# A decoder's expert layer: 96 gathered tokens on 128 partitions and 160 dense ones, in place of 128 and 128

## The chip, the cores and the metric

The kernel runs on one core of one Trainium2 chip. The metric is the device time of one launch in microseconds (us), the median of several runs. A profile of one execution shows the engines: TensorE (PE; its weight loads are PEld), VectorE (DVE), ScalarE (ACT), GpSimd (POOL) and SyncE (SP, which issues DMAs here). The 16 DMA engines serve two queues: SP's, with the weights, and GpSimd's, with the gathers.

## The reference, cut to what matters

Two decoder layers run over 256 tokens of width 1024. Each has four sequence mixers, a cross attention, and then the part that the change touches, product-key expert retrieval:

```python
def peer_ffn(h, w_q, sub_keys, expert_u, expert_v):   # on x = RMSNorm(h), 256 tokens
    q = (x @ w_q).reshape(t, 8, 2, 128)               # 8 heads, two half queries each
    s = einsum('thpd,hpkd->thpk', q, sub_keys)        # 16 lists of 128 scores per token
    s_top, i_top = top_k(s, 16)
    cand = s_top[:, :, 0, :, None] + s_top[:, :, 1, None, :]
    best_s, pos = top_k(cand, 16)                     # 16 of 16384 experts per head
    gate = softmax(best_s)
    act = gelu(x . expert_u[idx])                     # 128 rows of 4 KB per token
    return sum(act * gate * expert_v[idx])            # 128 more rows per token
```

A token so uses 128 of 16384 experts in each layer, a row of `expert_u` and a row of `expert_v` for each. Arithmetic is in float32.

## The kernel before, in words

Weights come through a `Stream`: units of 128 x 1024 floats (512 KB), loaded by SP into a ring of ten buffers. The first kind, the 154 units of projections per layer, is split into a rounded high part (ScalarE) and a low part (VectorE, the subtraction in `pump`), since each product is made of three rounded ones. The last 16 of them are the query projection of `peer`. The second kind, 128 units of `expert_u` and 128 of `expert_v` per layer, is used as it lands, in float32.

`peer(l)` treats the tokens in two ways. Tokens NG to 255 (NT of them) are dense: all 16384 experts are computed for them. `u_unit(j)` multiplies one up unit (stationary) with `xf` (moving, NT columns), `u_evac` puts the gelu into `Sx`, and `w_step` makes the weight of each expert for four tokens at a time, from two masks that a small matmul joins; `w_put` multiplies it into `Sx`. After 128 up units, `v_mm` runs 128 down units against `Sx`. The first NG tokens, one on each partition, are gathered: `issue()` has GpSimd fetch for each partition the row that `idx[:, n]` names, `g_step()` has VectorE multiply it with the token (`xg`) and sum, or, for rows of `expert_v`, scale and add it into `acc`. NS places take rows in turn, so a new gather waits for an old row to be used.

What is chosen comes from VectorE (`best`: two rounds of the eight largest of a list; `rects`: candidate sums; then masks that look up expert numbers). It is a generator, `retrieval()`. The program is written out in one order by a loop over 16 query units and 128 up units: after each unit a credit is added, and the generator is advanced until its `yield` values have used it up. So the yields set how far selection lies ahead of or behind the units in each engine's order, not when it runs: an engine runs its own list in order and waits for others through semaphores. From the first half's selection on, 0.85 `g_step`s are placed after each unit, and all others among the down units.

NG is 128 before: the first 128 tokens gathered, the last 128 dense. Lists of both halves are chosen first, 16 times two, then the candidates of the first half, then those of the second. When the last two units (HOLD) are done, `h` gets `acc` by one VectorE addition for the gathered tokens; the dense ones come back by transposes (`back_half`) and `resid`.

Of the kernel before, what the change touches and what calls it, by code (L numbers as in the profile page):

```python
# [46 lines left out]
NG = 128  # L47
NT = T - NG
NS = 12
# [12 lines left out]
class Stream:  # L62
# [3 lines left out]
    def __init__(self, nc, rawp, wp, lp, srcs):  # L66
        self.nc, self.srcs = nc, srcs
        self.pools = {"raw": (rawp, NRAW, F32), "whi": (wp, NHI, F32R), "wlo": (lp, NLO, F32R)}
        self.used = {"raw": [], "whi": [], "wlo": []}
        self.ring = ["raw"] * NRAW + ["wlo"] * NLO + ["whi"] * NHI  # L70
        self.more, self.turn = None, 0
        self.raw, self.hi, self.lo = {}, {}, {}
        self.a = self.b = self.c = self.i = self.done = 0
        self.start = {}
# [25 lines left out]
    def pump(self, hi, lo):  # L100
# [9 lines left out]
        while self.c < min(n, lo, self.b):  # L110
            if self.c not in self.start:
# [3 lines left out]
                self.nc.vector.tensor_tensor(t, self.raw.pop(self.c), self.hi[self.c].bitcast(F32), OP.subtract)  # L115
# [39 lines left out]
def decoder(ctx, tc, x, memt, wd, ut, pv, pu, fnb, prm, fing, skt, cst, idn, out, dbg=None, layers=L):  # L155
# [14 lines left out]
    S = Stream(nc, rawp, wp, wlp, units)  # L170

# [893 lines left out]
    def peer(l):  # L1065
# [17 lines left out]
        last, nsel = back, [0]  # L1083

        def own(n):
            if not nsel[0]:
                nsel.append(up.tile([128, 3664], F32, name="sel"))
            nsel[0] += n
            return nsel[1][:, nsel[0] - n:nsel[0]]
        sS = back(4096).rearrange("p (a b c) -> p a b c", a=2, b=16)  # L1090
        if NG == 128:
            back = own
# [12 lines left out]
        back = last  # L1105
# [8 lines left out]
        G.tensor_tensor(xf, xh.bitcast(F32)[:, :, NG:], xl.bitcast(F32)[:, :, NG:], OP.add)  # L1114
        xg = up.tile([128, D], F32, name="xg")
        acc = up.tile([128, D], F32, name="acc")
        G.dma_start(acc, fnb[l])
        defer(lambda: V.scalar_tensor_tensor(xg[:NG], h[:NG, 0], rs[:NG, 2:3], acc[:NG], op0=OP.mult, op1=OP.mult), 4)
# [5 lines left out]
        place = [rows[:NG, n] for n in range(NS - 4)]  # L1124

        def more_places():

            for n in ("xh", "xl"):
                t_ = xp.tile([128, 2, D], F32, name=n)
                place.extend(t_[:NG, i] for i in range(2))  # L1130
# [15 lines left out]
        def rects(lst, dst, p0, p1, o=0):  # L1146
            for a0, na, b0, nb in lst:
                ov = dst[:, :, o:o + na * nb]
                x0, x1 = p0[:, :, a0:a0 + na], p1[:, :, b0:b0 + nb]
                if na == 1:  # L1150
                    V.tensor_tensor(ov, x0.to_broadcast([128, 8, nb]), x1, OP.add)
                elif nb == 1:
                    V.tensor_tensor(ov, x0, x1.to_broadcast([128, 8, na]), OP.add)
                else:
                    V.tensor_tensor(ov.rearrange("p h (a b) -> p h a b", a=na),
                                    x0[:, :, :, None].to_broadcast([128, 8, na, nb]),
                                    x1[:, :, None, :].to_broadcast([128, 8, na, nb]), OP.add)
# [13 lines left out]

        def retrieval():


            for b in range(16):
                while scored["n"] <= b:
                    yield None
                best(*((sv[:, tt, b], su_[:, tt, b], sS[:, tt, b]) for tt in range(2)))
                yield 1.3
            for tt in range(2):  # L1180
                V.tensor_copy(si[:, tt], su_[:, tt])
                s4 = sv[:, tt].rearrange("p (h q) c -> p h q c", q=2)
                i4 = si[:, tt].rearrange("p (h q) c -> p h q c", q=2)
                V.tensor_scalar(i0s[:, tt], i4[:, :, 0], 128.0, None, op0=OP.mult)
                rects([(a, na, 0, nb) for a, na, nb, _ in CAND], cd, s4[:, :, 0], s4[:, :, 1])
                yield 1.2
                rects(PAYL, py, i0s[:, tt], i4[:, :, 1])
                yield 1.0
                for n in range(0, 8, 2):
                    best(*((bv[:, n + i], bp[:, n + i], cd[:, n + i]) for i in range(2)))  # L1190
                    V.tensor_copy(bf[:, n:n + 2], bp[:, n:n + 2])
                    yield 1.0

                    for h_ in (n, n + 1):
                        ms = []
                        for k0, nc_, m in ((0, NPAY, bm0), (8, NCAND, bm1)):
                            sh = [128, 8, nc_]
                            m = m.rearrange("p (k c) -> p k c", k=8)
                            ms.append((k0, nc_, m, sh))
                        for k0, nc_, m, sh in ms:  # L1200
                            V.tensor_tensor(m, pord[:, None, :nc_].to_broadcast(sh),  # L1201
                                            bf[:, h_, k0:k0 + 8, None].to_broadcast(sh), OP.is_equal)
                        for k0, nc_, m, sh in ms:
                            V.tensor_tensor(m, m, py[:, h_, None, :nc_].to_broadcast(sh), OP.mult)  # L1204
                        yield 1.5
                        for k0, nc_, m, sh in ms:
                            V.tensor_reduce(be[:, h_, k0:k0 + 8], m, AX.X, OP.add)  # L1207
                        yield 0.75
                V.tensor_scalar(bi, be, 1.0 / 128, -63.5 / 128, op0=OP.mult, op1=OP.add)
                V.tensor_scalar(bi, bi, 12582912.0, -12582912.0, op0=OP.add, op1=OP.add)  # L1210
                V.scalar_tensor_tensor(bf, bi, -128.0, be, op0=OP.mult, op1=OP.add)
                V.tensor_tensor(be, bv, bv[:, :, 0:1].to_broadcast([128, 8, 16]), OP.subtract)
                A.activation(be, be, AF.Exp)
                if not tt:
                    b2 = ga.rearrange("p (h c) -> p h c", h=8)
                    V.scalar_tensor_tensor(b2, bf, 128.0, bi, op0=OP.mult, op1=OP.add)
                    V.tensor_scalar(idx, ga, float(l * 16384), None, op0=OP.add)
                    more_places()
                    for _ in range(NS):
                        issue()  # L1220
                yield 0.9
                V.tensor_reduce(gs, be, AX.X, OP.add)  # L1222
                V.reciprocal(gs, gs)
                V.tensor_tensor(be, be, gs[:, :, None].to_broadcast([128, 8, 16]), OP.mult)
                yield 0.6
                if tt or NG < 128:
                    ps = four(wps())
                    for c, src in enumerate((bi, bf, be)):
                        PE.transpose(ps[:, c], src.rearrange("p h c -> p (h c)"), ident)
                if not tt:  # L1230
                    V.tensor_copy(gate, be.rearrange("p h c -> p (h c)"))
                if tt or NG < 128:
                    prog["wait"] = True
                    yield None
                    prog["wait"] = False
                if tt:
                    V.tensor_copy(slots[:, :, 128 - NG:], ps[:, :3])
# [356 lines left out]
```

## Time and profile before

| | us |
|---|---|
| median of 3 runs | 2436.06 |
| lowest, highest | 2434.64, 2437.12 |
| the profiled execution | 2435.94 |
| its span, first to last instruction | 2434.1 |
| TensorE (matmul) busy | 2123.2 |
| VectorE busy | 1680.4 |
| ScalarE busy | 846.8 |
| GpSimd busy | 705.5 |
| DMA moved | 711.29 MB |

Busy time of the whole span says little here, as the stages have different limits; the rows below go by stage. In them, a `f32` matmul of the program stands as two instructions, each with its weight load; one in rounded f32 as one. Names are the program's, with buffer numbers left out; one memory can carry several names (`whi`, `wlo` and `raw` are the ring's buffers, `xh` and `xl` also hold gathered rows).

### The profile page before, as it was taken

How to read it: one execution, taken by the hardware profiler on the slowest of the kernel's cores; microseconds unless marked ns; L12 is line 12 of the kernel's file. 1: busy time of each engine (PE TensorE's matmuls, PEld its weight loads, DVE VectorE, ACT ScalarE, POOL GpSimd, SP SyncE). 2: the span in 40 equal slices, each digit the busy share in tenths (PEclk: the TensorE clock that was granted, in tenths of full speed). 3: DMA queues.
4: the chain of work that ended last, by engine and by line, in shares of the span. 5: the costliest groups of instructions: out<-in, count | busy, mean ns of one | idle time of the engine just before them, and what ended most of it. 6: DMA issues, size and time to landing. Idle time of an engine off the chain costs nothing.

```text
span 2434.1 us, 41395 instructions
## 1 busy us (share of the span) xinstructions
PE 2123.2 (87%) x16010; PEld 1982.0 (81%) x16010; DVE 1680.4 (69%) x3591; ACT 846.8 (35%) x1729; POOL 705.5 (29%) x565
## 2 busy tenths in 40 slices
PE   8999999998888878778299999999989888887871
PEld 8898999898888877777299989998979888777771
DVE  7877776599766655455778777665997667454557
ACT  6756755531444200000067567554314442000000
POOL 1010000103443455555410100001045435555554
PEclk9999999999999999999699999999999999999996
DMA  6444455468999999999844544554689999999996
GB/s 209 151 156 156 156 176 179 143 221 332 409 409 409 408 409 409 409 409 409 319 165 158 159 147 160 174 182 149 241 334 408 408 408 408 409 409 409 409 409 265
DMA packets 195605, 711.29 MB, mean 292 GB/s; under 512 B 21712, under 2 KB 21968, under 8 KB 195152
## 3 DMA queue, kind: packets, MB, share of 16 engines
q1 hardware_dynamic: 120672, 434.47, 49.1%
q0 software_dynamic: 74736, 274.17, 28.5%
q8 instruction: 126, 2.06, 0.3%
q14 instruction: 71, 0.58, 0.1%
HBM read 707.51 MB, written 1.05 MB: 291 GB/s over the span
## 4 chain that ended last, share of the span: by engine, by line
PE 40%; DMA 39%; DVE 12%; issue 5%; POOL 2%; ACT 2%; DVEq 0%; POOLq 0%; SPq 0%; ACTq 0%
PE b L236 38%; DMA rows<-in_pv_dram,idx 14%; DMA wlo<-in_ut_dram 5%; DMA raw<-in_ut_dram 4%; DMA xh<-in_pv_dram,idx 4%; DMA whi<-in_ut_dram 3%; DMA xl<-in_pv_dram,idx 3%; DMA rows<-in_pu_dram,idx 3%; DVE acc L1270 3%; DVE sel L1170 1%; POOL rows L1251 1%; DVE sel L1201 1%; DVE sel L1204 1%; DVE rows L1261 1%; DVE sel L1207 1%
## 5 line engine op out<-in xcount | busy, mean ns | idle before, releaser
L107 ACT ACTIVATE whi<-raw 128x1024 fp32r<-128x1024 f32 x308 | 324.3, 1057 | 502.9 <-PE b L236 380.2
L115 DVE TENSOR_TENSOR wlo<-raw,whi 128x1024 fp32r<-128x1024 f32 x308 | 373.2, 1220 | 74.5 <-ACT whi L107 70.0
L1270 DVE SCALAR_TENSOR_TENSOR acc<-rows,aw,acc 128x1024 f32<-128x1024 f32 x168 | 215.8, 1285 | 174.1 <-DMA rows<-in_pv_dram,idx 172.9
L1251 POOL DMA_INDIRECT rows<-in_pu_dram,idx x176 | 213.3, 1212 | 396.7 <-DVE gs L1222 173.1
L236 PE MATMUL b<-xh,wlo 128*128 128x256 f32 x1120 | 317.4, 283 | 4.2 <-DVE wlo L115 4.0
L236 PE MATMUL b<-xh,whi 128*128 128x256 f32 x1120 | 321.0, 287 | 0.0
L236 PE MATMUL b<-xl,whi 128*128 128x256 f32 x1120 | 317.6, 284 | 1.0 <-DVE xl L313 0.9
L1251 POOL DMA_INDIRECT rows<-in_pv_dram,idx x168 | 226.0, 1345 | 178.7 <-DMA rows<-in_pv_dram,idx 75.2
L1261 DVE CUSTOM_DVE_ANT_0 rows<-rows,xg 128x1024 f32<-128x1024 f32 x176 | 213.3, 1221 | 60.9 <-DMA rows<-in_pu_dram,idx 60.9
L236 PE MATMUL b<-Sx,whi 128*128 128x128 f32 x1600 | 206.0, 282 | 52.4 <-DMA whi<-in_pv_dram 52.4
L236 PEld LDWEIGHTS b<-Sx,whi 128*128 128x128 f32 x1600 | 187.2, 192 | 71.0 <-DMA whi<-in_pv_dram 70.9
L236 PE MATMUL b<-xf,whi 128*128 128x128 f32 x1600 | 204.0, 286 | 43.7 <-ACT Sx L1336 27.2
L236 PEld LDWEIGHTS b<-xf,whi 128*128 128x128 f32 x1600 | 193.7, 200 | 51.6 <-ACT Sx L1336 28.0
L236 PEld LDWEIGHTS b<-xh,wlo 128*128 128x128 f32 x1120 | 214.5, 191 | 6.9 <-DVE wlo L115 6.9
L236 PEld LDWEIGHTS b<-xl,whi 128*128 128x128 f32 x1120 | 214.1, 191 | 1.9 <-DVE xl L313 1.7
L236 PEld LDWEIGHTS b<-xh,whi 128*128 128x128 f32 x1120 | 214.0, 191 | 0.5
L236 PE MATMUL b<-Sx,wlo 128*128 128x128 f32 x1248 | 162.0, 283 | 42.7 <-DMA wlo<-in_pv_dram 42.7
L285 POOL TENSOR_TENSOR rs<-rs,epsh 128x1 f32<-128x1 f32 x14 | 7.8, 555 | 658.8 <-DVE rs L283 658.8
L236 PEld LDWEIGHTS b<-Sx,wlo 128*128 128x128 f32 x1248 | 147.0, 193 | 57.5 <-DMA wlo<-in_pv_dram 56.0
L236 PE MATMUL b<-Sx,raw 128*128 128x128 f32 x1248 | 159.9, 282 | 38.6 <-DMA raw<-in_pv_dram 38.6
L236 PEld LDWEIGHTS b<-Sx,raw 128*128 128x128 f32 x1248 | 145.6, 192 | 52.8 <-DMA raw<-in_pv_dram 51.3
L257 ACT ACTIVATE Sx<-b 128x512 f32<-128x512 f32 (+17 forms) x100 | 40.1, 406 | 361.9 <-PE b L236 309.8
(316 smaller groups left out, 4354.8 us busy)
## 6 DMA issues: line engine op xcount, KB each, us to landing
raw<-in_wd_dram SPq DMA_DIRECT2D x308, 512.0 KB, 3.8
whi<-in_ut_dram SPq DMA_DIRECT2D x100, 512.0 KB, 20.4
whi<-in_pv_dram SPq DMA_DIRECT2D x100, 512.0 KB, 20.4
raw<-in_ut_dram SPq DMA_DIRECT2D x78, 512.0 KB, 19.9
wlo<-in_ut_dram SPq DMA_DIRECT2D x78, 512.0 KB, 20.4
raw<-in_pv_dram SPq DMA_DIRECT2D x78, 512.0 KB, 20.4
wlo<-in_pv_dram SPq DMA_DIRECT2D x78, 512.0 KB, 20.4
rows<-in_pu_dram,idx POOLq DMA_INDIRECT x176, 19.7
```

The lines of the kernel that those rows point to most:

```text
L107: self.nc.scalar.activation(t, self.raw[self.b], AF.Copy)
L115: self.nc.vector.tensor_tensor(t, self.raw.pop(self.c), self.hi[self.c].bitcast(F32), OP.subtract)
L236: PE.matmul(o, w, m, start=st, stop=sp)
L257: A.activation(o, i, AF.Copy)
L285: G.tensor_tensor(rs[:, 2 + tt:3 + tt], rs[:, tt:tt + 1], epsh[:, :1], OP.pow)
L1170: V.max_index(i[:, c], v[:, c], s)
L1201: V.tensor_tensor(m, pord[:, None, :nc_].to_broadcast(sh), bf[:, h_, k0:k0 + 8, None].to_broadcast(sh), OP.is_equal)
L1204: V.tensor_tensor(m, m, py[:, h_, None, :nc_].to_broadcast(sh), OP.mult)
L1207: V.tensor_reduce(be[:, h_, k0:k0 + 8], m, AX.X, OP.add)
L1251: G.indirect_dma_start(out=place[n % NS], out_offset=None, in_=src, in_offset=bass.IndirectOffsetOnAxis(ap=idx[:NG, n % 128:n % 128 + 1], ...
L1261: V.tensor_tensor_reduce(s, s, xg[:NG], 1.0, 0.0, OP.mult, OP.add, accum_out=act[:NG, k:k + 1])
L1270: V.scalar_tensor_tensor(acc[:NG], s, aw[:NG, k:k + 1], acc[:NG], op0=OP.mult, op1=OP.add)
```

## The change

NG becomes 96, so 96 tokens are gathered and 160 are dense. The gathered rows still come 128 at a time: partitions 96 to 127 take the last 32 of the 128 expert slots of tokens 0 to 95, in three groups of 32 tokens (`NX` = 3). So 96 gathers cover `expert_u` and 96 `expert_v`, in place of 128 and 128. `spread` copies the slots' numbers and gates over by small DMAs, `token_rows` copies the tokens, `acc` becomes three sums, and `add_sums` adds them to the right tokens by three matmuls with a constant (`join`) on top of the transposes. NS is 11. The selection tiles lie in the tail of `Sx`, no longer in a tile of their own, so that up units from the 53rd on need the selection done (`jsel`; it was 64).

The selection's order is new: lists of the first half, four heads at a time, each four followed by their candidates (`picks`); then the numbers of the first half, then lists and candidates of the second half. The yields have other values. In the query projection, the low parts of three units in four are made by GpSimd (`aside`), and `xf` is made by VectorE.

```diff
-NG = 128
+NG = 96
+NR = 128 - NG
+NX = NG // NR
 NT = T - NG
-NS = 12
+NS = 11
...
+                e = self.nc.gpsimd if self.c in self.aside else self.nc.vector
+                e.tensor_tensor(t, self.raw.pop(self.c), self.hi[self.c].bitcast(F32), OP.subtract)
...
+        q = l * (ND + 256) + ND - 16
+        S.aside.update(q + i for i in range(1, 16) if i % 4)
...
-        G.tensor_tensor(xf, xh.bitcast(F32)[:, :, NG:], xl.bitcast(F32)[:, :, NG:], OP.add)
+        V.tensor_tensor(xf, xh.bitcast(F32)[:, :, NG:], xl.bitcast(F32)[:, :, NG:], OP.add)
...
+        def token_rows():
+            V.scalar_tensor_tensor(xg[0][:NG], h[:NG, 0], rs[:NG, 2:3], xg[1][:NG], op0=OP.mult, op1=OP.mult)
+            for u in range(1, NX):
+                act_copy(xg[u][:NG], xg[0][:NG])
+            for u in range(NX):
+                G.dma_start(xg[u][NG:], xg[0][NR * u:NR * u + NR])
+        defer(token_rows, 4)
...
+        def spread(t_):
+            for u in range(NX):
+                G.dma_start(t_[NG:, NR * u:NR * u + NR], t_[NR * u:NR * u + NR, NG:])
...
+            for h0 in (0, 4):
+                for b in range(2 * h0, 2 * h0 + 8, 2):
+                    while scored["n"] <= b + 1:
+                        yield None
+                    lists(0, b)
+                    yield 3.4
+                yield from picks(0, h0, h0 + 4)
+            yield from numbers(0)
+            V.tensor_copy(h8(gate, 16)[:NG], be[:NG])
+            spread(gate)
+            prog["tt"] = 1
+            for b in range(0, 16, 2):
+                if b == 6:
+                    ps = turned(0)
+                if b == 10:
+                    V.tensor_copy(slots[:, :, :128 - NG], ps[:, :3, NG:])
+                lists(1, b)
+                yield 3.4
+            yield from picks(1, 0, 8)
+            yield from numbers(1)
+            yield 1.2
+            yield 1.2
+            yield 1.2
+            ps = turned(1)
+            yield 1.2
+            V.tensor_copy(slots[:, :, 128 - NG:], ps[:, :3])
+            prog["r"] = NT
+            prog["tt"] = 2
...
+            k = n % NG
+            G.indirect_dma_start(out=place[n % NS], out_offset=None, in_=pu if n < NG else pvr,
+                                 in_offset=bass.IndirectOffsetOnAxis(ap=idx[:, k:k + 1], axis=0))
...
+            u = k // NR
+            if n < NG:
+                V.tensor_tensor_reduce(s, s, xg[u], 1.0, 0.0, OP.mult, OP.add, accum_out=act[:, k:k + 1])
...
+                if k % NR == 0:
+                    V.tensor_scalar(acc[u], s, aw[:, k:k + 1], None, op0=OP.mult)
+                else:
+                    V.scalar_tensor_tensor(acc[u], s, aw[:, k:k + 1], acc[u], op0=OP.mult, op1=OP.add)
...
-            credit += 2.2 if not prog["tt"] else 1.1
+            credit += 2.2 if not prog["tt"] else 1.2
...
-        V.tensor_tensor(h[:NG, 0], h[:NG, 0], acc[:NG], OP.add)
...
+        def add_sums(b):
+            for u in range(NX):
+                mm(tb[b][0], join[:, u], acc[u][:, 512 * b:512 * b + 512], False, u == NX - 1)
```

On GpSimd, at the start of the first layer's `peer`, this stood before: the load of the sub keys, the making of `xf`, the load of the norm's gain, and then the gathers.

```order
L1109 DMA Sx<-in_skt_dram 128x2048
L1114 TENSOR_TENSOR xf<-xh,xl 128x1024
L1117 DMA acc<-in_fnb_dram 128x1024
L1251 DMA rows<-in_pu_dram,idx 128x1024 x8
L1251 DMA xh<-in_pu_dram,idx 128x1024 x2
```

Now there are the twelve low parts (`wlo`) and, among them, the copies of the tokens' rows; the copies of `idx` precede the first gather.

```order
L1106 DMA Sx<-in_skt_dram 128x2048
L1117 DMA xg_5318<-in_fnb_dram 128x1024
L1118 DMA join<-in_jn_dram 128x384
L118 TENSOR_TENSOR wlo<-raw,whi 128x1024 x3
L1125 DMA xg_5317<-xg_5317 32x1024
L1125 DMA xg_5318<-xg_5317 32x1024
L1125 DMA xg_5319<-xg_5317 32x1024
L118 TENSOR_TENSOR wlo<-raw,whi 128x1024 x9
L1142 DMA idx<-idx 32x32 x3
L1286 DMA rows<-in_pu_dram,idx 128x1024 x7
```

Twelve subtractions have come to this queue, ahead of every gather, and one addition has left it.

On VectorE, at the same place, the query units' low parts stood between the selection of lists before; `xl` is the last of the norm, and MAX, MAX_INDEX and MATCH_REPLACE belong to the lists.

```order
L313 SCALAR_TENSOR_TENSOR xl<-b_5268,pr,xh 128x256 x2
L115 TENSOR_TENSOR wlo<-raw,whi 128x1024 x4
L1118 SCALAR_TENSOR_TENSOR xg<-h,rs,acc 128x1024
L115 TENSOR_TENSOR wlo<-raw,whi 128x1024
L1168 MAX sel<-Sx 128x8 x2
L1170 MAX_INDEX sel<-sel,Sx 128x8 x2
L1166 MATCH_REPLACE Sx<-sel,Sx 128x128 x2
```

After the change the same place reads:

```order
L320 SCALAR_TENSOR_TENSOR xl<-b_5268,pr,xh 128x256 x2
L1111 TENSOR_TENSOR xf<-xh,xl 128x1280
L118 TENSOR_TENSOR wlo<-raw,whi 128x1024
L1121 SCALAR_TENSOR_TENSOR xg_5317<-h,rs,xg_5318 96x1024
L1181 MAX Sx<-Sx 128x8 x2
L1183 MAX_INDEX Sx<-Sx 128x8 x2
L1179 MATCH_REPLACE Sx<-Sx 128x128 x2
```

`xf` has come from GpSimd, and one low part in four is left.

On TensorE, at the end of the first layer, the last down units (`Sx,wlo`) were followed by transposes of the dense tokens (`idt,Sx`, line 1418) and the next layer's norm (line 304).

```order
L236 MATMUL b_8607<-Sx,wlo 128x128 x4
L1418 MATMUL b_10202<-idt,Sx 128x128 x4
L236 MATMUL b_8608<-Sx,wlo 128x128 x4
L1418 MATMUL b_10215<-idt,Sx 128x128 x4
L304 MATMUL b_10231<-idt,Sx 128x128 x2
```

Now the moving side of the units has 160 columns, the transposes are matmuls for both halves of the tokens, and the three sums are joined to them.

```order
L243 MATMUL b_8762<-Sx,wlo 128x160 x4
L243 MATMUL b_10233<-idt,Sx 128x128 x4
L243 MATMUL b_10238<-idt,Sx 128x128 x4
L243 MATMUL b_8763<-Sx,wlo 128x160 x4
L243 MATMUL b_10238<-xg_5317,join 128x512
L243 MATMUL b_10238<-xg_5318,join 128x512
L243 MATMUL b_10238<-xg_5319,join 128x512
L243 MATMUL b_10251<-idt,Sx 128x128 x4
L243 MATMUL b_10256<-idt,Sx 128x128 x4
L243 MATMUL b_10256<-xg_5317,join 128x512
L243 MATMUL b_10256<-xg_5318,join 128x512
L243 MATMUL b_10256<-xg_5319,join 128x512
```

Sixteen transposes' worth of matmuls and six joins stand where eight transposes stood.

## Rows read from the trace of the kernel before

**Rows 1.** Stages of layer 1: start:end us, width, busy us (count), clock, DMA, GB/s.

```profile
477.00:533.00 56.00, 54.20 (x441) 52.98 (x442) 49.45 (x216) 22.85 (x33) 6.65 (x3) 1.00 0.55 179
533.00:560.00 27.00, 27.00 (x245) 27.00 (x244) 26.08 (x160) 6.29 (x12) 0.00 (x0) 1.00 0.97 361
560.00:625.00 65.00, 51.02 (x404) 50.21 (x403) 63.87 (x234) 9.72 (x19) 29.31 (x27) 0.86 0.92 353
625.00:842.00 217.00, 197.63 (x1667) 190.06 (x1667) 147.10 (x359) 86.88 (x279) 91.82 (x79) 1.00 1.03 409
842.00:1170.00 328.00, 261.12 (x2045) 237.37 (x2044) 169.64 (x172) 1.03 (x4) 183.53 (x132) 1.00 1.03 409
1170.00:1208.00 38.00, 1.18 (x7) 0.59 (x5) 34.55 (x27) 2.66 (x4) 20.55 (x19) 0.54 0.89 349
1208.00:1221.00 13.00, 6.48 (x31) 5.87 (x31) 5.85 (x11) 4.63 (x13) 1.13 (x2) 0.64 0.12 41
```

**Rows 2.** Timeline of TensorE, first down units: start, length in us, what.

```profile
842.58 3.74 PE L236 MATMUL b<-Sx,whi 128*128 128x128 f32 x32
```

**Rows 3.** TensorE's groups by shape: stationary, moving, count, busy us, mean ns, idle.

```profile
L236 PE MATMUL b<-xh,wlo 128*128 128x256 f32 x1120 | 317.4, 283 | 4.2 <-DVE wlo L115 4.0
L236 PE MATMUL b<-wlo,xh 128*128 128x512 f32 x288 | 112.7, 391 | 0.0
L236 PE MATMUL b<-bb,aa 128*128 128x128 f32 x512 | 67.8, 275 | 0.5 <-ACT Sx L257 0.5
L236 PE MATMUL b<-cph,bch 128*128 128x128 f32 x4 | 0.9, 224 | 0.0
```

**Rows 4.** The page's costliest groups: the sums of gathered down rows on VectorE.

```profile
L1270 DVE SCALAR_TENSOR_TENSOR acc<-rows,aw,acc 128x1024 f32<-128x1024 f32 x168 | 215.8, 1285 | 174.1 <-DMA rows<-in_pv_dram,idx 172.9
```

**Rows 5.** Timeline of TensorE in the mixers: 256 columns, then 8 columns.

```profile
49.39 0.28 PE L236 MATMUL b<-xl,whi 128*128 128x256 f32 x1
49.51 0.28 PE L236 MATMUL b<-xh,wlo 128*128 128x256 f32 x1
49.63 0.51 PE L236 MATMUL b<-loga,ct 128*128 128x8 f32 x4
```

**Rows 6.** Waits in layer 1's expert part: total us, times, longest us.

```profile
PE b L236 <- ACT Sx L1336: 13.0, 2, 7.7
PE b L236 <- ACT gt L1339: 4.8, 8, 0.6
DVE Sx L1340 <- ACT gt L1339: 55.3, 34, 4.6
```

**Rows 7.** Timeline: picks of the first half begin, its indices, the first gather.

```profile
543.05 0.27 DVE L1181 CAST sel<-sel 128x256 f32<-128x256 uint32 x1
...
571.92 0.23 DVE L1217 TENSOR_SCALAR idx<-ga 128x128 uint32<-128x128 f32 x1
572.44 1.02 POOL L1251 DMA_INDIRECT rows<-in_pu_dram,idx  x1 [86.27 <-DVE gs L1222]
```

**Rows 8.** Timeline of layer 1's end: residual, next layer's first product.

```profile
1213.57 1.39 DVE L273 TENSOR_TENSOR h<-h,b 128x512 f32<-128x512 f32 x2
...
1220.95 0.36 PE L236 MATMUL b<-xh,whi 128*128 128x256 f32 x1
```

**Rows 9.** Timeline at the query's start: VectorE's subtractions beside GpSimd's addition.

```profile
479.90 3.48 DVE L115 TENSOR_TENSOR wlo<-raw,whi 128x1024 fp32r<-128x1024 f32 x3
...
480.14 5.51 POOL L1114 TENSOR_TENSOR xf<-xh,xl 128x1024 f32<-128x1024 f32 x1 [2.45 <-DVE xl L313]
```

**Rows 10.** VectorE's groups by shape, 625 to 842 us.

```profile
L1261 DVE CUSTOM_DVE_ANT_0 rows<-rows,xg 128x1024 f32<-128x1024 f32 x50 | 60.7, 1221 | 8.9 <-DMA rows<-in_pu_dram,idx 8.9
L1293 DVE TENSOR_SCALAR aa<-idt,slots 128x128 f32<-128x128 f32 x128 | 36.5, 359 | 0.0
...
L1261 DVE DVE_READ_ACCUMULATOR2_ANT act<- 128x1 f32 x77 | 6.4, 83 | 0.0
L1340 DVE TENSOR_TENSOR Sx<-Sx,gt 128x240 f32<-128x240 f32 x2 | 0.8, 409 | 3.3 <-ACT gt L1339 3.3
```

More of the change, by code (lines that the diff above doesn't have):

```diff
@@ L73, in __init__ @@
         self.a = self.b = self.c = self.i = self.done = 0
-        self.start = {}
+        self.start, self.aside = {}, set()
         for k, (_, whole) in enumerate(srcs):
@@ L170, in decoder @@
     S = Stream(nc, rawp, wp, wlp, units)
+    for l in range(layers):
+        q = l * (ND + 256) + ND - 16
+        S.aside.update(q + i for i in range(1, 16) if i % 4)
     h = base.tile([128, 2, D], F32, name="h")
@@ L1123, in peer @@
         rows = sp.tile([128, NS - 4, D], F32, name="rows")
-        place = [rows[:NG, n] for n in range(NS - 4)]
+        place = [rows[:, n] for n in range(NS - 4)]
         def more_places():
@@ L1129, in more_places @@
                 t_ = xp.tile([128, 2, D], F32, name=n)
-                place.extend(t_[:NG, i] for i in range(2))
+                place.extend(t_[:, i] for i in range(2))
+        def spread(t_):
+            for u in range(NX):
+                G.dma_start(t_[NG:, NR * u:NR * u + NR], t_[NR * u:NR * u + NR, NG:])
         scored = {"n": 0}
@@ L1146, in rects @@
         def rects(lst, dst, p0, p1, o=0):
+            n = dst.shape[1]
             for a0, na, b0, nb in lst:
@@ L1170, in best @@
                     V.max_index(i[:, c], v[:, c], s)
-        def retrieval():
[L1175 to L1237, printed above, removed]
-                    prog["r"] = NT
-                elif NG < 128:
-                    V.tensor_copy(slots[:, :, :128 - NG], ps[:, :3, NG:])
-                prog["tt"] = tt + 1
-                yield 0.5
@@ new lines, in numbers @@
+        def numbers(tt):
+            V.tensor_scalar(bi, be, 1.0 / 128, -63.5 / 128, op0=OP.mult, op1=OP.add)
+            V.tensor_scalar(bi, bi, 12582912.0, -12582912.0, op0=OP.add, op1=OP.add)
+            V.scalar_tensor_tensor(bf, bi, -128.0, be, op0=OP.mult, op1=OP.add)
+            if not tt:
+                V.scalar_tensor_tensor(h8(ga, 16)[:NG], bf[:NG], 128.0, bi[:NG], op0=OP.mult, op1=OP.add)
+                V.tensor_scalar(idx[:NG], ga[:NG], float(l * 16384), None, op0=OP.add)
+                spread(idx)
+                more_places()
+                for _ in range(NS):
+                    issue()
+            V.tensor_tensor(be, bv, bv[:, :, 0:1].to_broadcast([128, 8, 16]), OP.subtract)
+            A.activation(be, be, AF.Exp)
+            yield 1.2
+            V.tensor_reduce(gs, be, AX.X, OP.add)
+            V.reciprocal(gs, gs)
+            V.tensor_tensor(be, be, gs[:, :, None].to_broadcast([128, 8, 16]), OP.mult)
+            yield 0.6
@@ L1333, in u_evac @@
                 while prog["tt"] < 2:
-                    next(gen)
+                    next(gen, None)
             if tb < NT:
@@ L1428, in peer @@
                 back_half(0)
-        def whole(b, tt, over=None):
-            if tt or NG < 128:
-                resid(b, tt, tb[b][tt], scr, over)
-                return
-            square(junk[b], tt, b)
-            if b:
-                over(tt)
-        junk = [flat(ys[b])[:, :512] for b in range(2)]
+        add_sums(0)
+        back_half(1)
+        add_sums(1)
         for tt in (1, 0):
-            whole(0, tt)
-        back_half(1)
+            resid(0, tt, tb[0][tt], scr)
         def put(tt, r):
@@ L1497, in shape_constants, with joins @@
     return arr, np.ascontiguousarray(idn)
+def joins():
+    o = np.zeros((128, NX, 128), np.float32)
+    for u in range(NX):
+        for p in range(128):
+            o[p, u, p if p < NG else NR * u + p - NG] = 1.0
+    return o
 def lay_out(i):
```

110 lines of the change are left out of this document (66 added, 44 removed).

## The prediction

> **What bounds the kernel now.** I read the stages first [rows 1]: each layer's expert part has five. The query projection (477 to 533 us) keeps TensorE busy 54 of 56 us. Then come 128 up units and 128 down units of 512 KB, and beside them 256 gathers of 128 rows of 4 KB, again 512 KB each. From 625 to 1170 us the DMA engines are full, at 409 GB/s. The reader is to see that TensorE is not full there: in the down stretch (842 to 1170) it ran 2045 matmul instructions, 128 units of 16, so a unit took 328/128 = 2.56 us. That is 2 x 524,288 bytes at 409 GB/s: one unit and one gather, half the DMA each, although 2045 instructions need less. Next the timeline of that stretch [rows 2]: with its data there, TensorE does 32 instructions in 3.74 us; less the 0.275 us that the last one takes [rows 3], they start 3.465/31 = 112 ns apart, 1.79 us a unit. DMA therefore sets this stretch. Then 1170 to 1208: TensorE is at 1.2 of 38 us, VectorE at 34.6. About 27 gathered rows are left when the units end, and they are added up one at a time, 1.285 us each [rows 4]. 13 us later the next layer starts. The other layer repeats this within a few us.
>
> **The change, part by part.** Durations are from the profiled execution, 2435.9 us, 0.1 us below the median of 2436.06, so its sums are used as they stand.
>
> *Fewer gathers, wider matmuls.* 64 of 256 gathers go per layer: 64 x 1.28 = 82 us of DMA. The dense units now stream 160 columns, not 128. What an instruction of 160 columns costs is the largest term, and no row shows one. The 112 ns are not the columns': a matmul of 8 columns takes four instructions in 0.51 us, the last three also 112 ns apart [rows 5], so loading 128 x 128 weights sets it. So the cost could stay at 112. But an f32 instruction of 128 columns ends 275 ns after its start, like a rounded-f32 one of 256 columns (283), while a rounded one of 128 takes 224 [rows 3]. 256 columns more cost 391 - 283 = 108 ns. So f32 columns count double, and 128 of them need 108 ns, just under the weight load; 160 are 64 more column times, 27 ns, so 112 + 27 = 139 ns. From above: 256 single columns follow each other at 120 ns [rows 5], hence 120 + 27 = 147. I take 138.5, as 112 is already a ceiling for 128. A unit is then 16 x 138.5 = 2.216 us. (The Trainium skill, "FP8 and Floating Point Precision", TensorE Precision Notes, has true f32 in four passes through the array, two for each of the two instructions here. By that rule 139 holds and the time is the forecast; by the flat 112 it would be 2245. The lengths in rows 3 side with the rule, though none is of 160 columns.)
>
> *Up units.* 128 x 2.216 = 283.6 us. The dense tokens' weights come in groups of four: 40 groups for 160 tokens in place of 32, 8 instructions each, 40 x 8 x 0.112 = 35.8. TensorE's waits: today 13.0 us for ScalarE in two stalls, where an exponential stands in ScalarE's order before VectorE has its input, and 4.8 for evacuation [rows 6]. The new yields let the program run behind VectorE, so I take the 13 away. The 4.8 I raise to 7, since the groups are crowded into the last 73 units (now 88), and I put 3 on the second half's selection. Sum 329 us, against 842 - 533 = 309. DMA does not limit this stretch: 0.85 gathers and one unit are 2.37 us, TensorE needs 2.216 + 0.28.
>
> *When the selection must be done.* Its scratch lies in the last part of Sx, so all selection must be out before unit 53 is evacuated: TensorE gets there at 533 + 55 x 2.216 = 655. VectorE: candidate picks of one half take 572 - 543 = 29 us [rows 7]; for the first half, half of them now lie in the query stretch, so the gathers start about 533 + 14 + list work and index copies = 560, not 572. SP's unit loads share the DMA with them 12 us sooner, at 2.56 us a unit against TensorE's 2.216; the ring of 10 units carries that. In VectorE's order 28 gathered rows stand before the last 14 us of the second selection: 560 + 28 x 2.56 + 14 = 646. Nine us to spare, hence only 3 us of cost; from below 0, from above 20 if the gathers start late.
>
> *Down units.* The program consumes 0.85 rows a unit from the 37th of 144 units (query units counted) on: 91 by now. 11 are in flight, 90 are left. While they run, DMA splits as today: 90 x 2.56 = 230 us, in which 90 units land and up to 10 wait in the ring: 100, and TensorE would take 104. The other 28 go at 2.216: 62. Sum 292, I take 294 (ring empty 314, TensorE alone 284), against 328.
>
> *The end.* All gathers are in some 50 us before the last unit, so VectorE's chain goes and TensorE is late next. After its last unit come transposes as f32 matmuls, 16 instructions x 0.112 = 1.8, three joins of 512 f32 columns (1024 column times each instruction, 6 x 0.44 = 2.6), for both halves 8.8; then from the residual to the next layer 1220.95 - 1213.57 = 7.4 us as today [rows 8]. 16 us, against 1221 - 1170 = 51.
>
> *Low parts on GpSimd.* 12 of 16 query units per layer move. VectorE needs 1.16 us each, and it has 49 of 56 us to do there [rows 1, 9]. GpSimd's only op of this size took 5.51 us [rows 9]. At that, 12 are 66 us in a stretch of 56, and the query gets 15 us longer. But that op ran beside three VectorE subtractions that began before it and ended at 479.90 + 3.48 = 483.38; it ended at 485.65, 2.3 us later. I take 2.3: 27 us in 56, with a start 1.5 us later since the first is needed at once. Queued behind them on GpSimd are three row copies and the index copies, then every gather. (The Trainium skill, "SBUF — State Buffer", Who interferes with whom, says that a VectorE instruction with two SBUF inputs and a GpSimd one that reads SBUF fully block each other. By it the 5.51 is 3.2 of waiting and the time is the forecast, but VectorE's own picks will be held up by GpSimd too; with 5.5 as the op's own time it would be 2372.)
>
> *Sum per layer:* +1.5 +20 (329 - 309) -34 (294 - 328) -35 (16 - 51) = -47. Twice: 2436 - 94 = 2342 us. At 147 ns, 4096 instructions a layer add 33 us: -14, 2408. With the ring full and no waits, -67: 2302.
>
> **Rivals.** *VectorE becomes the bound after the selection.* All weight groups fall into the last 73 up units. VectorE has there 63 gathered rows x 1.30 = 82 us, 160 x 36.5/128 = 46 for the weights' masks, 76 products of half a us (0.41 in the row) = 38 [rows 10]: 166, and TensorE 198 + 7. Against: 40 us of room. For: VectorE waited 55.3 us for ScalarE's evacuation in 34 waits [rows 6]; if each of 36 pairs still costs 1.6 and gathers 14, VectorE takes 238, +33 a layer; with a selection 20 us late as well the layer is 6 us longer than before: 2448. It decides from 47 us a layer on.
>
> *Columns are free.* The instruction stays at 112 ns. Then DMA bounds: up units (128 + 102) x 1.28 = 295, down 230 + 28 x 1.79 = 280, end 16: 591 + 1.5 against 688, twice 95.5 less: 2245. Against it: 275 beside 224.
>
> *GpSimd needs 5.5 us.* +15 a layer: 2372. For it stands the row as printed; against it the 2.3 us.
>
> **How the numbers follow.** Forecast 0.68, own range 2302 to 2408, for the two prices of the instruction. VectorE bound 0.13, columns free 0.06, GpSimd slow 0.08 (inside the forecast's range), other 0.05. Range 2300 to 2420: it leaves out the free columns and most of the VectorE case. About 0.2% is what a measurement here can tell. Faster: 0.68 + 0.06 + 0.08 and a quarter of the rest, 0.86. Slower 0.12, same 0.02.
>
> **What would show it.** Dense instructions 139 ns apart: right; 112 or 147 and more: that term is wrong. GpSimd's subtractions near 2.3 us, the query under 60 us. No wait of TensorE at unit 53. TensorE busy nearly throughout up and down stretch, DMA under 409 GB/s in the last third of the down stretch, no VectorE chain at the end. Wrong would be: TensorE waiting for DMA through the down stretch, or for evacuation by more than 20 us in the up stretch.

## The result and the profile after

The changed kernel takes 2337.73 us, median of 4 runs (2336.17 to 2339.8), the kernel before 2435.84 in 4; the ratio is 0.9598, 95% interval 0.9581 to 0.9614. It is 98 us faster; forecast were 94 (2342 us, range 2300 to 2420). The total is right; the parts are less so:

| layer 1's expert part, us | before | forecast change | after | change |
|---|---|---|---|---|
| first up unit starts | 532.85 | +1.5 | 530.85 | -2.0 |
| up units | 309.9 | +20 | 323.3 | +13.4 |
| down units | 327.9 | -34 | 304.9 | -23.0 |
| end, to the next layer's first product | 50.5 | -35 | 11.1 | -39.4 |
| sum | | -47 | | -51 |

(In the kernel before, eight instructions of the last unit stand behind the chain of sums; they are counted with the end.) The other layer gained 46: up units 324.4, down units 305.6.

The stages of layer 1 after the change; the columns are those of [rows 1], with which they are to be compared.

```profile
476.50:531.00 54.50, 53.55 (x444) 52.93 (x443) 40.30 (x145) 24.82 (x36) 33.72 (x18) 1.00 0.60 205
531.00:566.00 35.00, 35.00 (x262) 35.00 (x261) 29.17 (x159) 6.03 (x11) 2.94 (x5) 1.00 0.87 287
566.00:660.00 94.00, 88.67 (x643) 87.98 (x642) 83.16 (x335) 15.81 (x32) 46.78 (x41) 0.97 1.02 404
660.00:854.00 194.00, 194.00 (x1483) 194.00 (x1482) 142.26 (x364) 101.35 (x309) 68.84 (x63) 1.00 0.99 377
854.00:1077.00 223.00, 215.29 (x1482) 202.38 (x1481) 117.91 (x100) 0.65 (x2) 126.23 (x91) 1.00 1.03 409
1077.00:1159.00 82.00, 81.16 (x587) 79.39 (x587) 12.06 (x11) 2.99 (x4) 0.00 (x0) 1.00 0.75 277
1159.00:1170.00 11.00, 8.67 (x44) 5.40 (x42) 4.38 (x9) 4.75 (x12) 1.30 (x2) 1.00 0.00 0
```

TensorE, the first busy column, is now busy nearly throughout, and its granted clock holds (0.86, 0.54 and 0.64 in the three stretches of [rows 1] in which TensorE stood idle, 0.97 at worst here). VectorE's chain at the end is gone: 4.38 us of work in the last 11, where it had 34.55 in 38. One stretch is still full of DMA with TensorE waiting in it: 854 to 1077, in which 215 of 223 busy us overstate TensorE: its 1482 instructions are worth 202 us at the 136 ns found below.

TensorE's timeline after the change: the stop at unit 53, then 64 dense instructions in one piece and the end of the layer.

```profile
656.06 0.80 PE L1244 MATMUL b<-idt,Sx 128*128 128x128 f32 x2 [4.26 <-DVE Sx L1224]
657.94 0.48 PE L1244 MATMUL b<-idt,Sx 128*128 128x128 f32 x1 [1.08 <-DVE Sx L1238]
...
1113.47 8.86 PE L243 MATMUL b<-Sx,whi 128*128 128x160 f32 x64
...
1155.86 1.95 PE L243 MATMUL b<-idt,Sx 128*128 128x128 f32 x16
1157.64 1.25 PE L243 MATMUL b<-Sx,wlo 128*128 128x160 f32 x8
1158.73 2.74 PE L243 MATMUL b<-xg,join 128*128 128x512 f32 x6
1161.30 1.95 PE L243 MATMUL b<-idt,Sx 128*128 128x128 f32 x16
1163.09 2.74 PE L243 MATMUL b<-xg,join 128*128 128x512 f32 x6
1168.16 1.94 PE L311 MATMUL b<-idt,Sx 128*128 128x128 f32 x16 [2.33 <-DVE Sx L301]
1170.00 0.38 PE L243 MATMUL b<-xh,whi 128*128 128x256 f32 x1
```

64 instructions of 160 columns in 8.86 us, less 0.30 for the last: 8.56/63 = 136 ns apart, forecast 138.5, where [rows 2] had 112 for 128 columns. The joins cost nearly what was forecast (six instructions of 512 columns in 2.74 us, forecast 2.6).

### The profile page after: what moved, and what is told of

The parts are those of the page before. It is cut to its first block, busy times and chain, and to the rows that moved or that the text cites. A ratio compares the mean times of both kernels' runs of the same rounds, so it can differ in the third digit from the quotient of the medians.

```text
span 2337.0 us, 41618 instructions
## 1 busy us (share of the span) xinstructions
PE 2280.6 (98%) x16216; PEld 2170.3 (93%) x16216; DVE 1545.3 (66%) x3483; ACT 890.7 (38%) x1813; POOL 591.5 (25%) x481
## 4 chain that ended last, share of the span: by engine, by line
PE 70%; DMA 21%; DVE 6%; ACT 1%; POOL 1%; issue 1%; SPq 0%; DVEq 0%; ACTq 0%; POOLq 0%
PE b L243 68%; DMA whi<-in_pv_dram 7%; DMA wlo<-in_pv_dram 5%; DMA raw<-in_pv_dram 3%; DMA xl<-in_pu_dram,idx 2%; DMA rows<-in_pu_dram,idx 2%; DMA xh<-in_pu_dram,idx 1%; DVE Sx L1212 1%; DVE Sx L1183 1%; DVE Sx L1215 1%; DVE Sx L1218 1%; PE b L509 0%; POOL rows L1286 0%; ACT whi L109 0%; DVE Sx L1181 0%
## 5 line engine op out<-in xcount | busy, mean ns | idle before, releaser
L1308 DVE SCALAR_TENSOR_TENSOR xg<-rows,aw,xg 128x1024 f32<-128x1024 f32 x120 | 154.2, 1285 | 140.7 <-DMA rows<-in_pv_dram,idx 140.2
L243 PE MATMUL b<-Sx,whi 128*128 128x160 f32 x1600 | 233.0, 302 | 5.8 <-DMA whi<-in_pv_dram 0.2
L243 PEld LDWEIGHTS b<-Sx,whi 128*128 128x128 f32 x1600 | 219.4, 190 | 18.0 <-DMA whi<-in_pv_dram 17.9
L243 PE MATMUL b<-xf,whi 128*128 128x160 f32 x1600 | 225.2, 299 | 0.0
L1286 POOL DMA_INDIRECT rows<-in_pv_dram,idx x122 | 166.7, 1366 | 142.4 <-DMA rows<-in_pv_dram,idx 60.8
L1286 POOL DMA_INDIRECT rows<-in_pu_dram,idx x126 | 140.5, 1115 | 220.3 <-DVE act L1297 137.7
L243 PE MATMUL b<-Sx,wlo 128*128 128x160 f32 x1248 | 181.8, 302 | 7.3 <-DMA wlo<-in_pv_dram 3.3
L264 ACT ACTIVATE Sx<-b 128x512 f32<-128x512 f32 (+21 forms) x116 | 43.2, 376 | 377.8 <-PE b L243 351.6
L243 PE MATMUL b<-Sx,raw 128*128 128x160 f32 x1248 | 181.4, 302 | 4.2
L243 PE MATMUL b<-xf,wlo 128*128 128x160 f32 x1248 | 180.5, 302 | 0.2 <-DMA wlo<-in_ut_dram 0.2
```

The costliest lines, as they stand in the source:

```text
L243: PE.matmul(o, w, m, start=st, stop=sp)
L264: A.activation(o, i, AF.Copy)
L1286: G.indirect_dma_start(out=place[n % NS], out_offset=None, in_=pu if n < NG else pvr, in_offset=bass.IndirectOffsetOnAxis(ap=idx[:, k:k + ...
L1308: V.scalar_tensor_tensor(acc[u], s, aw[:, k:k + 1], acc[u], op0=OP.mult, op1=OP.add)
```

## The experiments

All edits are to the changed kernel; its time is 2337.73, and "before" ran beside each at 2436 to 2438 us. The first four runs have one time each, the others five; a ratio is to "before", with its 95% interval. Only the first two leave something out, part of the output.

**What a column costs.** Two runs.

```
-                mm(ps[:, j % 2, :NT], unit[:, k], xf[:, k], k == 0, k == KC - 1)
+                w = 128 if k else NT
+                mm(ps[:, j % 2, :w], unit[:, k], xf[:, k, :w], k == 0, k == KC - 1)
...the down units in the same way; the other run with 144
```

128 columns: 

> The changed kernel, but of the 160 dense columns only 128 go through TensorE in the expert units (the first instruction pair of each accumulation excepted); the output of 32 tokens is left out. Gathers, selection and everything else stay. Columns theory (f32 columns count double, 112 ns of weight load is the floor): the instruction falls from 136 to 112 ns, TensorE is no longer the bound, DMA is: up stretch about 295 us (323 with 160 columns), down stretch 223 + 37 units x 1.79 = 290 (305), so 2337 - 2 x 43 = about 2250 us. Rival (the 136 ns come from something other than the number of columns, such as where the columns lie in Sx): instruction stays at 136, time stays at 2337.

144 columns: 

> The same with 144 columns (16 tokens left out). Columns theory, linear at 0.85 ns a column: instruction 122 to 124 ns; up stretch about 300 us, down stretch 297; about 2337 - 2 x 31 = 2275 us. Rival, a step rather than a slope: 136 ns as with 160 columns and 2337 us, or 112 ns as with 128 and the time of that run.

Measured: 2290.53 and 2295.54 us. TensorE's timeline in the down stretch, first with 128 columns:

```profile
1097.56 7.31 PE L243 MATMUL b<-Sx,whi 128*128 128x128 f32 x64
```

With 144:

```profile
1096.91 8.00 PE L243 MATMUL b<-Sx,whi 128*128 128x144 f32 x64
```

Less 0.28 for the last, over 63: 112 and 122.5 ns. With 136 for 160 columns that is a slope of 0.84 ns a column, and 112 at 128 where the slope alone would give 109: the columns theory, floor included. The times came out 40 and 20 us above the expectations, and the stages with 128 columns say why:

```profile
531.00:831.00 300.00, 284.00 (x2385) 277.28 (x2385) 254.29 (x859) 122.60 (x352) 121.67 (x108) 0.99 1.01 396
831.00:1053.00 222.00, 176.90 (x1377) 160.48 (x1377) 117.88 (x100) 0.22 (x1) 126.10 (x91) 1.00 1.03 409
1053.00:1135.00 82.00, 78.61 (x688) 77.28 (x689) 11.99 (x10) 2.88 (x4) 0.44 (x1) 1.00 0.85 312
```

The up stretch fell from 323 to 299 nearly as expected (295), but the down stretch stayed: 304.2 us against 304.9 (299.5 with 144 columns), although TensorE needs 24 ns less for each instruction. While gathers run, units land no faster than gathers do; a faster TensorE only waits longer (busy 177 of 222 us).

**How much room VectorE has.** Two runs.

```
+                    for _ in range(2):
                         V.tensor_scalar(aa[:, k], iota, slots[:, 0, t:t + 1], slots[:, 2, t:t + 1], ...)
...the other run with range(3)
```

Masks twice: 

> The changed kernel with every mask of the dense tokens' weights (128x128 on VectorE) made twice: 160 more instructions of 0.285 us, 46 us more of VectorE per layer, all after the selection. The prediction put the point from which VectorE decides at 47 us a layer; in the trace of the changed kernel VectorE is busy 142 of 194 us there, 52 us of room. Room theory: hardly longer, 0 to 10 us a layer from waits, 2337 to 2357 us. Rival (the order of VectorE's instructions, not the sum, decides: evacuations stand behind gathered rows): most of the 46 us show, 2337 + 2 x 35 = about 2405.

Masks three times: 

> The same with every mask made three times: 91 us more of VectorE per layer. Room theory: 91 - 52 = 39 us a layer and what the waits add, 2337 + 78 to 98 = 2415 to 2435 us. Rival with the order deciding: 2337 + 2 x 80 = about 2500.

Measured: 2368.07 and 2495.15 us. The stretch from the first weights to the last up unit, and TensorE's waits in it, masks twice:

```profile
660.00:868.00 208.00, 199.34 (x1492) 196.73 (x1492) 198.13 (x525) 99.04 (x316) 73.62 (x63) 0.99 0.95 350
```

```profile
PE b L243 <- ACT Sx L264: 8.5, 8, 1.9
```

Masks three times:

```profile
660.00:932.00 272.00, 221.88 (x1491) 215.95 (x1490) 257.19 (x685) 98.66 (x316) 73.22 (x63) 0.91 0.77 269
```

```profile
PE b L243 <- ACT Sx L264: 48.5, 22, 4.4
```

VectorE's busy time grew by 56 and 115 us (142 in the changed kernel), not by 46 and 91: 160 masks were priced at the 0.285 us that 36.5/128 gives in [rows 10], but that row's mean is 0.359, and they add at that. With 56 more VectorE is full (198 of 208) and the up stretch is 13 us longer; the next 59 cost 64, and VectorE's waits for ScalarE's evacuations, 47.8 us in the changed kernel, are used up with masks three times:

```profile
DVE Sx L1379 <- ACT gt L1378: 1.3, 2, 0.7
```

Both times are above the room theory's ranges, which rest on the low price of a mask; the second even meets the rival's 2500, but the first is 37 us below the rival's 2405. So VectorE decides beyond about 50 us of added work a layer, the room that 142 of 194 in the profile leaves, and the sum decides rather than the order.

**Low parts on GpSimd.**

```
-        S.aside.update(q + i for i in range(1, 16) if i % 4)
+        S.aside.update(())
```

> The changed kernel with all low parts of the query units on VectorE, none on GpSimd. The prediction's step: 12 x 1.16 = 14 us go back to VectorE in the query stretch, the first half's picks and the first gather come about that much later (564 to 575 us or more), and the end of the selection, for which TensorE already waits 5 us, too: up to +10 us a layer, 2340 to 2357 us. Rival (VectorE and GpSimd hold each other up: beside GpSimd's subtractions VectorE's addition of 128x1280 took 7.22 us, and other instructions of 0.2 to 0.8 us took 1.2 to 3): what VectorE gets back in subtractions it saves in waiting; first gather within 3 us of 564, 2337 +- 4 us.

Measured: 2343.44 us, ratio to before 0.9614 (0.9600 to 0.9627), which overlaps the changed kernel's interval: 6 us slower at most a hint. The time lies in the first expectation's range and just outside the rival's, but what the first rests on, a later first gather, did not come; the rival's core holds. GpSimd's timeline with the subtractions on GpSimd (the changed kernel):

```profile
478.88 7.12 POOL L118 TENSOR_TENSOR wlo<-raw,whi 128x1024 fp32r<-128x1024 f32 x3
...
564.27 1.05 POOL L1286 DMA_INDIRECT rows<-in_pu_dram,idx  x1 [2.12 <-DMA idx<-idx]
```

VectorE's, in the same kernel:

```profile
480.13 7.22 DVE L1111 TENSOR_TENSOR xf<-xh,xl 128x1280 f32<-128x1280 f32 x1
...
515.47 2.25 DVE L1195 TENSOR_SCALAR Sx<-Sx 128x64 f32<-128x64 f32 x1
...
522.29 2.94 DVE L1212 TENSOR_TENSOR Sx<-idt,Sx 128x160 f32<-128x160 f32 x2
...
526.57 0.79 DVE L1212 TENSOR_TENSOR Sx<-idt,Sx 128x160 f32<-128x160 f32 x2
```

VectorE's, with all low parts on VectorE:

```profile
480.24 1.49 DVE L1111 TENSOR_TENSOR xf<-xh,xl 128x1280 f32<-128x1280 f32 x1
481.64 3.49 DVE L118 TENSOR_TENSOR wlo<-raw,whi 128x1024 fp32r<-128x1024 f32 x3
...
516.81 0.20 DVE L1195 TENSOR_SCALAR Sx<-Sx 128x64 f32<-128x64 f32 x1
```

GpSimd's, in that kernel:

```profile
562.96 1.04 POOL L1286 DMA_INDIRECT rows<-in_pu_dram,idx  x1 [0.47 <-DMA idx<-idx]
```

Alone, the addition takes 1.49 us; beside GpSimd it takes 7.22 and ends 1.35 us after GpSimd's third subtraction. A step of 0.20 us takes 2.25 beside a later subtraction, and two additions (line 1212) that take 0.79 us at 526.57 take 2.94 at 522.29. The first gather came at 562.96 us without GpSimd's help, at 564.27 with it: moving the low parts brought the gathers no sooner.

**The order of the selection.**

```
+            for b in range(0, 16, 2):
...
+                lists(0, b)
+                yield 3.4
+                lists(1, b)
+                yield 3.4
+            yield from picks(0, 0, 8)
...in place of lists and picks of the first half in two parts, and of the second half's lists later
```

> The changed kernel with the lists of both halves made before the picks of the first half, as in the kernel before; the rest of the order stays. The first gather comes some 25 us later (about 590 us), some 10 gathered rows move from the up stretch to the down stretch. If the start of the gathers counts one for one: +25 us a layer, 2387. If DMA is late only while gathers and units share it: 10 rows x (2.48 - 2.176) = +3 us a layer, and the selection ends no later, so 2337 to 2347 us. Rival on the other side: without gathered rows between its lists VectorE ends the selection sooner and TensorE's wait at unit 53 goes: -5 us a layer, 2327.

Measured: 2340.87 us, ratio 0.9606 (0.9593 to 0.9619): no difference that can be told from the changed kernel. The first gather comes 11 us later, at 575.08 us, not 25; the down stretch is 307.3 us (+2.4), the up stretch 322.5 (-0.8), and TensorE no longer stops at unit 53 (it has 2.9 us of another stop, told of below). Both of the last two theories show in part, and cancel.

**Gathers that wait for TensorE.** The wait is a write to a column of Sx that TensorE has just read.

```
             k = n % NG
+            if gq["v"] is not None:
+                G.memset(Sx[:, gq["v"], 0:1], 0.0)
             G.indirect_dma_start(out=place[n % NS], ...)
...
                 v_mm(j, unit, c)
+            gq["v"] = j
             acg += gr
```

> The changed kernel, but in the down stretch GpSimd writes one dead column of Sx before each gather, so that a gather is issued only when TensorE has finished the unit beside which it stands in the program (0.84 gathers a unit). Nothing is left out. In the changed kernel TensorE is idle some 26 us of the down stretch (305 us against 128 x 2.176 = 278.5), all of it while gathers come at 2.48 us each and take half the DMA. Sharing theory: paced gathers leave the units what TensorE needs; the demand is (1 + 0.84) x 1.28 = 2.36 us a unit against 2.176, the ring of ten units pays most of the difference, 5 to 10 us of idle are left; -16 to -20 us a layer, about 2300 us. Rival (the idle comes from the ring itself, a unit's load being issued too late): no change, 2337. A second rival: later gathers leave VectorE a chain at the end, +10 us a layer, 2357.

Measured: 2320.16 us (2318.99 to 2322.07), ratio 0.9521 (0.9508 to 0.9534); down stretches 295.9 us. Neither rival holds, but the gain is 9 us a layer, half of what the theory expected. Then slower, at 0.73 a unit, with the wait and without:

```
-        gr = (2 * NG - gq["n"]) / (nv - 6.0)
+        gr = (2 * NG - gq["i"]) / (nv - 2.0)
```

With the wait: 

> As the run with gathers that wait for TensorE, but with fewer gathers a unit: 90 over 124 units, 0.73 in place of 0.84. That run gave 2320 us: the down stretch 296 us in place of 305, TensorE still 17 us above its 278.5, DMA full to 1105 us. Sharing theory: at 0.73 the demand is 1.73 x 1.28 = 2.21 us a unit against TensorE's 2.176, 4 us over 124 units, which the ring pays; down stretch about 285 us, -10 us a layer, about 2300. Rival (a gather in flight takes its half of the DMA whenever it is issued, so that only the number of rows counts): 2320. Rival on the other side: the last sums come after the last unit, +5 us a layer, 2325 to 2330.

Without: 

> The control: the same order of instructions as with 0.73 gathers a unit, but GpSimd does not wait for TensorE. If the wait does it, the order alone changes nothing: VectorE and GpSimd have nothing else to do there and run ahead, 2337 +- 3 us. If the order does it, 2300 as with the wait.

Measured: 2311.46 (0.9484, 0.9471 to 0.9497) and 2352.51 us (0.9657, 0.9644 to 0.9670). The two differ by the wait alone, which is worth 41 us here. The paced one is the sharing theory, but for layer 1, whose down stretch took 300.3 us where layer 2's took 282.3; and the control missed by 15 us, 13 of them in layer 1's down stretch. One cause does both. VectorE's timeline at layer 1's end, paced at 0.73:

```profile
1107.11 1.28 DVE L1310 SCALAR_TENSOR_TENSOR xg<-rows,aw,xg 128x1024 f32<-128x1024 f32 x1 [2.93 <-DMA rows<-in_pv_dram,idx]
1136.18 1.23 DVE L118 TENSOR_TENSOR wlo<-raw,whi 128x1024 fp32r<-128x1024 f32 x1 [27.79 <-DMA raw<-in_wd_dram]
1137.33 1.28 DVE L1310 SCALAR_TENSOR_TENSOR xg<-rows,aw,xg 128x1024 f32<-128x1024 f32 x1
...
1150.41 0.48 DVE L1468 COPY Sx<-b 128x320 f32<-128x320 f32 x1
```

TensorE's timeline there:

```profile
1150.95 2.93 PE L243 MATMUL b<-idt,Sx 128*128 128x128 f32 x12 [12.32 <-DVE Sx L1468]
```

The slower rate leaves ten sums for after the loop, and in VectorE's order these stand behind the low part of the next layer's first unit, whose load waits for the ring. VectorE stands still for 27.8 us, does its ten sums, and TensorE waits 12.3 us for the copy behind them. The control's TensorE stops there too, though its last gather was issued at 1077.6:

```profile
1169.25 2.93 PE L243 MATMUL b<-idt,Sx 128*128 128x128 f32 x12 [11.25 <-DVE Sx L1465]
```

So the control's order was not harmless: it put the last sums where they wait. The next runs set this right and take the selection's wait.

**The selection's end and the last sums.**

```
-            credit += 2.2 if not prog["tt"] else 1.2
+            credit += 2.2 if not prog["tt"] else 1.7
```

Alone: 

> The changed kernel with one number altered: the second half's selection is written at 1.7 us a unit between the up units, not 1.2. This measures by itself what the selection's deadline at unit 53 cost in the change. In the changed kernel TensorE waited 4.3 + 1.1 us there, and the prediction put 3 us on it. If the wait is all: -5 us a layer, about 2327 us. With the paced kernels the same edit took the up stretch from 324 to 317 us, so if it is worth as much without pacing: -8 us a layer, about 2321. Rival (rows put off in the up stretch come back in the down stretch, where DMA is late): -2 us a layer, 2333.

With the paced kernel at 0.73: 

> The paced kernel with 0.73 gathers a unit, and the second half's selection written earlier between the up units (1.7 us of it a unit in place of 1.2). In the changed kernel TensorE waited 5.3 us at unit 53 for the end of that selection, in the paced one 1.0 us. If that wait is the selection's length: -1 to -5 us a layer against the paced kernel of the same call. Rival (gathered rows in the up stretch are put off by as much as the selection gains, and come back as rows of the down stretch): 0 to +3 us a layer.

And with the sums drained six units before the end:

```
+            if j == nv - 6:
+                while gq["n"] < 2 * NG:
+                    g_step()
```

> The paced kernel with 0.73 gathers a unit and the earlier selection (2296 us), but the last eleven sums of gathered rows are written before the next layer's first low part, not behind it. In the runs before, VectorE stood idle from 1107 to 1136 us in front of that low part, which needs a load that waits for the last units, and then did eleven sums of 1.3 us while TensorE waited 12.3 us for the copy behind them; the last layer, which has no next one, did not. Order theory: 12 us less, once, about 2284. Rival (the last gathers land late because the next layer's loads share the DMA): 2296.

Measured: alone 2338.61 us (0.9595, 0.9582 to 0.9608), no change; with pacing 2295.64 (0.9420, 0.9407 to 0.9433), 16 us less than the same kernel without the earlier selection, more than was expected: its up stretches are 317 us in place of 324. With the sums drained it is 2294.82 (0.9417, 0.9404 to 0.9430), not the 12 less. That edit does what it should: layer 1's down stretch is 284.6 us in place of 299.4. But both up stretches went from 317 to 322, and layer 2's down stretch from 283 to 286. The stop at unit 53 is gone in all three; in two of them another has come, as TensorE's timeline shows (selection alone):

```profile
575.69 0.30 PE L243 MATMUL b<-xf,whi 128*128 128x160 f32 x1 [0.81 <-issue]
...
578.52 0.30 PE L243 MATMUL b<-xf,whi 128*128 128x160 f32 x1 [1.72 <-issue]
```

Some 4 us in five pieces, just when the first eleven gathers are issued. No unit that came late explains them: the pieces lie between instructions of one unit, and VectorE, in the midst of a list, and ScalarE stand still too. Both go on with TensorE at 580.0 us, as their timelines show (selection alone):

```profile
576.40 0.09 DVE L1183 MATCH_VALUE_LOAD Sx<-Sx 128x8 f32 x1 [1.10 <-DVE Sx L1181]
...
579.26 0.09 DVE L1183 MATCH_VALUE_LOAD Sx<-Sx 128x8 f32 x1 [1.85 <-remote]
...
580.00 0.44 ACT L1374 ACTIVATE Sx<-b 128x320 f32<-128x320 f32 x1 [9.59 <-remote]
```

The DMA queues from 570 to 582 us, gathers (q0) and unit loads (q1), with packets, MB and share of the engines, selection alone:

```profile
q0 software_dynamic: 1058, 3.86, 80.4%
q1 hardware_dynamic: 290, 1.05, 21.9%
```

The changed kernel:

```profile
q0 software_dynamic: 689, 2.50, 52.3%
q1 hardware_dynamic: 640, 2.36, 49.1%
```

In ten of the kernels I compared this stretch: where gathers have 52 to 54% TensorE has no such stop (four kernels), where they have 76 to 83% (six) it does. The share is rather the effect of the stop than its cause. From 571 to 573.5 us, before TensorE stops, the gathers have 60.2% with the selection alone and 58.2% in the changed kernel. From 576 to 580 us, selection alone, the unit loads have next to nothing:

```profile
q0 software_dynamic: 456, 1.66, 101.8%
q1 hardware_dynamic: 8, 0.01, 0.6%
```

SP, which issues them, issued none between 569.5 and 580.0 us, though TensorE used up units until 574.9. What stops these engines in some kernels and not in others stays open; no run changed it alone.

## Why the prediction was right, and where not

**The columns: right.** 139 ns forecast, 136 measured; the slope and the floor are shown by the runs with 128 and 144 columns. The Trainium skill ("FP8 and Floating Point Precision", TensorE Precision Notes) has true f32 in four passes through the array, which makes two for each of the two instructions here; the measured 0.84 ns a column agree, twice the 108/256 = 0.42 of a rounded column in [rows 3].

**Up units: 323, forecast 329.** 5 us less are the price (2048 x 2.5 ns), 7 the waits for evacuation, of which TensorE had none. The stop at unit 53 cost 5.3 us, forecast 3: the first gather came at 564, not 560, and the selection ended at 658, not 646, so the nine us to spare were not there. TensorE waits for it at 651.8, three us sooner than forecast, because it starts sooner and its units are cheaper. Some 4 us were in no term, slower instructions right behind the stop among them (16 in 3.77 us, where 16 take 2.34). The forecast's sign, no wait there, failed; by the two paced kernels at 0.73 the late selection costs 7 to 8 us a layer in the up stretch.

**Down units: 305, forecast 294. This step failed in part.** I let ninety units land beside ninety gathers and added ten that wait in the ring. The queues from 854 to 1077 us, in the same columns:

```profile
q1 hardware_dynamic: 12611, 45.93, 51.7%
q0 software_dynamic: 12351, 44.99, 50.6%
```

At 524,288 bytes that is 87.6 units and 85.8 gathers, half each as forecast. (The Trainium skill, "DMA: Bandwidth & Descriptors", Queues, rings and completion order, has each DMA engine take queues in turn, a packet at a time; this stretch agrees, with 12611 packets of one queue and 12351 of the other.) TensorE started 1482 instructions there, 92.6 units, so only 5 of them came out of a stock, where I had counted on ten: the ring's loads were issued but mostly not yet landed (20.4 us from issue to landing, 8 units' time at 2.56). The other 35.4 units take 77 us at 2.176; with 2 for the first half's transposes and 3 of waiting that is 82, and 223 + 82 = 305. The sign of being wrong, TensorE waiting for DMA through the down stretch, so came true for a tenth of the first 223 us. The gathers that run beside the units therefore set the first part, whatever TensorE costs: the run with 128 columns took 304.2. My rival with free columns, 2245 us, was too low for the same reason; the run with the columns at that price took 2290.

**The end: 11, forecast 16.** The terms were nearly right (joins 2.74 twice, transposes 1.95 twice), but the first half's transposes, at 1155.86, stand before the last unit's own instructions, and from the last join, at 1165.8, to the next layer's product are 4.2 us, where I had taken the 7.4 of [rows 8].

**Low parts: the price right, the use not.** GpSimd's subtractions take 7.12/3 = 2.37 us in a row, forecast 2.3, and the query stretch did not grow. But VectorE saved 12 x 1.16 us of subtractions and lost 5.7 on one addition alone, which the prediction had not priced. (By the Trainium skill, "SBUF — State Buffer", Who interferes with whom, the two engines shut each other out; the 7.22 against 1.49 us agree; that VectorE waited through three subtractions in a row is this trace's.) It cost nothing because VectorE was idle 14 of 54.5 us there.

**VectorE did not become the bound.** Its waits for ScalarE's evacuations, on which that rival rested, are still there, in the stretch from 660 to 854 us:

```profile
DVE Sx L1378 <- ACT gt L1377: 47.8, 28, 3.1
```

1.7 us each, as it said, but they lie in VectorE's 52 us of room. The forecast's 40 and the point of 47 us stand near the 50 that the mask runs show.

So the total came out within 5 us because the errors have both signs: +11 a layer in the down stretch, -7 in the up stretch, -4 at the end, -3.5 at the query. That they nearly cancel is luck.

**What is better than both kernels.** Gathers paced by TensorE at 0.73 a unit, the earlier selection, and the last sums before the next layer's low part: 2294.82 us, 0.9417 of the kernel before where the change is at 0.9598, 43 us below it. Its stages from 853 us, the last gathers among them:

```profile
853.00:1100.00 247.00, 247.00 (x1821) 247.00 (x1820) 112.78 (x96) 0.65 (x2) 104.37 (x165) 1.00 1.03 407
```

TensorE has no gap left where it had lost a tenth of its instructions to the sharing.

## What to carry to other kernels

When two queues share a full DMA, a byte that is needed now and one that is needed 80 us later counted alike here: the one whose consumer has time must be held back by that consumer's pace, or the other engine starves while the total looks balanced. A buffer counts as stock only when its data has landed. And an engine's program order is a queue too: whatever stands behind a step that waits for the next stage waits with it, so a stage's last work is written before the next stage's first.

## What the runs showed of the hardware that was not expected

A VectorE addition beside three consecutive subtractions on GpSimd waited through all three (7.22 us for 1.49), not only through the one under way. And in six of ten kernels TensorE, VectorE, ScalarE and SP stood still together for some microseconds while the first eleven gathers were issued, though the burst itself is the same in all of them; the trace names no cause.
